# Seven block products instead of eight in other chunks of the feed-forward parts of a two-layer hybrid block

## The chip, the cores and the metric

The kernel runs on one core of one Trainium2 chip. The metric is the device time of one execution in microseconds, as a median of several runs. It has five engines that matter here: TensorE (PE, with its weight loads shown as PEld), VectorE (DVE), ScalarE (ACT), GpSimd (POOL, hardly used) and SyncE (SP), which issues the transfers.

## What is computed

Two layers work on two streams of 256 tokens each (the latent and the context) with a width of 1024. A layer has a feed-forward part, a mixer of three branches and a second feed-forward part. Every part is preceded by a normalization whose shift, scale and gate come from a conditioning vector (`ada_w`). Cut to the parts that the change touches:

```python
def swiglu(h, w1, w3, w2):
    return (jax.nn.silu(h @ w1) * (h @ w3)) @ w2
...
for l in range(DEPTH):
    ml = (sc @ ada_w[l] + ada_b[l]).reshape(B, 1, N_MOD, D_MODEL)
    mc = (scc @ ada_w[l] + ada_b[l]).reshape(N_MOD, D_MODEL)
    xl = xl + 0.5 * ml[:, :, 2] * swiglu(ln_mod(xl, ...), ffn_w1[l, 0], ffn_w3[l, 0], ffn_w2[l, 0])
    xc = xc + 0.5 * mc[2] * swiglu(ln_mod(xc, ...), ffn_w1[l, 0], ffn_w3[l, 0], ffn_w2[l, 0])
    yl, yc = token_mixer(...)
    xl = xl + ml[:, :, 5] * yl
    xl = xl + 0.5 * ml[:, :, 8] * swiglu(ln_mod(xl, ...), ffn_w1[l, 1], ffn_w3[l, 1], ffn_w2[l, 1])
    ...
```

`h @ w1` and `h @ w3` go from 1024 to 2816 columns, `w2` goes back. All arithmetic is in fp32.

## The kernel before

Activations lie transposed: 128 features on the partitions, 512 columns for the tokens of both streams (the first 256 latent, `LAT`, the others context, `CTX`). Every fp32 operand of the large products is split into a high and a low part of the faster type fp32r, and a product takes three matmuls (high by high, high by low, low by high). The splitting of weights is done on the chip: ScalarE casts the high part (line 253 or 662), VectorE subtracts it (line 254 or 663).

A feed-forward part (`ffn`, line 708, named here by layer and part as (0,0), (0,1), (1,0) and (1,1)) goes over the 22 chunks of 128 columns of `w1` and `w3` in three thirds (`THIRDS`, line 25: chunks 0 to 7, 8 to 14, 15 to 21). A chunk ends with silu, product and split into `gh` and `gl`; after each third follow its downs, eight products with `w2` that are added to `x`. The last downs of a part go by stream, so that the next normalization can begin.

A normal chunk loads its weights (`load13`), splits them and multiplies 8 blocks of 128 rows of `w1` and `w3` by all 512 columns: 2 x 8 x 3 = 48 matmuls of 512 columns. The other form (`seven`, line 652) regards `w1`, `w3`, the two halves of the inner dimension and the two streams as 2 by 2 blocks and takes seven block products instead of eight: 7 x 4 x 3 = 84 matmuls of 256 columns. For that VectorE makes block sums of the weights in place (line 674), each of the seven blocks is split anew (lines 662 and 663), and the results are combined on VectorE. The block sums of the moving operand (`seven_sums`, line 634) are made once in a part; the code calls it three chunks (`SUMS`) ahead of the first seven, and the results are given back after the last one. They take 16 of the 27 tiles (`W_FFN`) in which split weights are held; one more holds the junk output of line 394.

`SEVEN` (line 37) says which chunks take that form. Three of the four parts have such chunks.

The modulation of later stages is computed beside the feed-forward parts by VectorE: `ada_steps` (line 377) multiplies tiles of `ada_w`, 512 KB each, by the conditioning vector and sums along the columns (line 394), for each tile once per stream, with two tiles in flight. These steps are handed out by `feed`: in normal chunks that aren't the last of their third, two rates' worth, and in each down of the first two thirds, one rate. The rate divides the number `FEEDS` of a part (42, 40, 40 tiles) by the number of these places (`ups`, line 715, counts the chunks). `lazy` gives the steps a priority 300 places later than their place in the code.

PE's order is that of the code (line 97). On the other engines and on SP a planner orders the instructions at build time by priority and by when it holds their operands to be ready; each engine then works through its list in order.

```python
units = SEVEN.get((l, j), ())
ups = sum(m not in units and m < b - 1 for a, b in THIRDS for m in range(max(a, 3), b))
rate = FEEDS.get((l, j), 0) / (2 * ups + 16)
```

Of the kernel before, what the change touches and what calls it, by code (L numbers as in the profile page):

```python
# [33 lines left out]
FEEDS = {(0, 0): 42, (0, 1): 40, (1, 0): 40}  # L34


SEVEN = {(0, 0): range(8, 16), (0, 1): range(8, 16), (1, 0): range(8, 22)}
SUMS = 3
PREP = 3
LATER = 300  # L40
# [48 lines left out]
def body(ctx, tc, ins, out):  # L89
# [618 lines left out]
    def ffn(l, j, streams, order, after, first, ahead, prep=None):  # L708
# [4 lines left out]
        filled = False  # L713
        units = SEVEN.get((l, j), ())
        ups = sum(m not in units and m < b - 1 for a, b in THIRDS for m in range(max(a, 3), b))
# [1045 lines left out]
```

## Time and profile before

| | us |
|---|---|
| median of 3 runs (2202.43 to 2210.25) | 2202.67 |
| the profiled execution | 2201.5 |
| its span, from the first to the last instruction | 2199.7 |
| PE busy in the span | 2139.0 (97%) |
| DVE busy | 1642.8 (75%) |
| ACT busy | 1121.1 (51%) |
| mean granted clock of TensorE | 0.995 |

A busy time is the union of the durations of an engine's instructions. Matmuls overlap in the records, so the pace of a row of them is read from the length of a stretch and not from the single duration. [...]

### The profile page before, as it was taken

What the parts mean: (1) busy time and instruction counts of PE and PEld (TensorE: products, weight loads), DVE (VectorE), ACT (ScalarE), POOL (GpSimd) and SP (SyncE); (2) the same over time, 40 slices, a digit from 0 to 9 for tenths busy, and PEclk for the clock granted to TensorE, in tenths of its full rate; (3) what the DMA queues carried; (4) which work ended last, traced back from release to release, by engine and by line L of the source; (5) the groups of instructions that cost most, each with busy time, mean ns of one, the idle gap of its engine ahead of it and who ended that gap; (6) DMA issues with size and microseconds to landing.
All of it is one profiled execution on the core that took longest, in us unless ns stands there. A gap on an engine that the chain in (4) does not pass through costs nothing.

```text
span 2199.7 us, 35090 instructions
## 1 busy us (share of the span) xinstructions
PE 2139.0 (97%) x13405; PEld 1877.3 (85%) x13405; DVE 1642.8 (75%) x3455; ACT 1121.1 (51%) x2265; POOL 26.7 (1%) x59
## 2 busy tenths in 40 slices
PE   6999899999999999999989999999999999999999
PEld 5778888977787778998888889899999778999999
DVE  6899994568776644699997359797785987868664
ACT  4425443558676533442344344245454878757553
POOL 0000000000000000000000000000000000000000
PEclk9999999999999999999999999999999999999999
DMA  9563463311122333336535324753242222454652
GB/s 361 189 230 137 163 222 104 111 67 63 68 62 92 103 100 104 117 134 221 174 124 180 126 87 145 252 188 106 96 154 95 66 99 82 149 188 167 234 190 95
DMA packets 73658, 310.44 MB, mean 141 GB/s; under 512 B 6929, under 2 KB 10513, under 8 KB 59025
## 3 DMA queue, kind: packets, MB, share of 16 engines
q1 hardware_dynamic: 73488, 308.19, 40.1%
q8 instruction: 105, 1.72, 0.3%
q14 instruction: 65, 0.52, 0.1%
HBM read 303.97 MB, written 4.19 MB: 140 GB/s over the span
## 4 chain that ended last, share of the span: by engine, by line
PE 82%; DVE 10%; ACT 4%; DMA 2%; issue 1%; POOL 0%; SPq 0%; ACTq 0%; DVEq 0%; POOLq 0%
PE dn L268 6%; PE dn L269 6%; PE dn L270 6%; PE p L268 6%; PE p L269 6%; PE p L270 6%; PE pg L268 3%; PE pg L269 3%; PE pg L270 3%; PE pj L268 2%; PE pj L269 2%; PE pj L270 2%; PE pa L669 2%; DVE wlo L663 2%; PE pa L667 2%; PE pa L668 2%
## 5 line engine op out<-in xcount | busy, mean ns | idle before, releaser
L253 ACT CAST whi<-raw 128x512 fp32r<-128x512 f32 x724 | 431.5, 610 | 551.0 <-PE p L269 160.5
L254 DVE TENSOR_TENSOR wlo<-raw,whi 128x512 fp32r<-128x512 f32 x724 | 480.0, 675 | 259.1 <-ACT whi L253 177.9
L268 PE MATMUL dn<-gh,whi 128*128 128x512 f32 (+1 forms) x809 | 275.6, 341 | 0.0
L269 PE MATMUL dn<-gl,whi 128*128 128x512 f32 (+1 forms) x809 | 275.1, 340 | 0.0
L270 PE MATMUL dn<-gh,wlo 128*128 128x512 f32 (+1 forms) x809 | 275.0, 340 | 0.0
L394 DVE SCALAR_TENSOR_TENSOR junk<-ada,cb 128x1024 bf16<-128x1024 f32 x208 | 253.6, 1219 | 26.6 <-DMA ada<-ada 25.1
L268 PE MATMUL p<-hh,whi 128*128 128x512 f32 (+1 forms) x736 | 256.3, 348 | 0.0
L269 PE MATMUL p<-hl,whi 128*128 128x512 f32 (+1 forms) x736 | 256.1, 348 | 0.1
L270 PE MATMUL p<-hh,wlo 128*128 128x512 f32 (+1 forms) x736 | 255.7, 347 | 0.0
L662 ACT CAST whi<-raw 128x512 fp32r<-128x512 f32 x210 | 129.7, 621 | 149.0 <-DVE raw L674 56.3
L270 PEld LDWEIGHTS dn<-gh,wlo 128*128 128x128 f32 x809 | 152.2, 188 | 18.7
L269 PEld LDWEIGHTS dn<-gl,whi 128*128 128x128 f32 x809 | 152.1, 188 | 18.6
L268 PEld LDWEIGHTS dn<-gh,whi 128*128 128x128 f32 x809 | 152.1, 188 | 18.6
L268 PEld LDWEIGHTS p<-hh,whi 128*128 128x128 f32 x736 | 138.4, 188 | 20.8 <-ACT whi L253 0.8
L268 PE MATMUL pj<-hh,whi 128*128 128x512 f32 (+1 forms) x400 | 154.2, 385 | 1.9 <-DVE li L941 1.9
L270 PEld LDWEIGHTS p<-hh,wlo 128*128 128x128 f32 x736 | 138.4, 188 | 19.4
L269 PEld LDWEIGHTS p<-hl,whi 128*128 128x128 f32 x736 | 138.4, 188 | 19.2 <-DVE hl L495 0.3
L663 DVE TENSOR_TENSOR wlo<-raw,whi 128x512 fp32r<-128x512 f32 x210 | 140.1, 684 | 12.0 <-ACT whi L662 11.8
L269 PE MATMUL pj<-hl,whi 128*128 128x512 f32 (+1 forms) x400 | 144.0, 360 | 0.0
L270 PE MATMUL pj<-hh,wlo 128*128 128x512 f32 (+1 forms) x400 | 143.7, 359 | 0.0
L268 PE MATMUL pg<-hh,whi 128*128 128x512 f32 (+1 forms) x384 | 130.0, 339 | 0.0
L269 PE MATMUL pg<-hl,whi 128*128 128x512 f32 (+1 forms) x384 | 129.7, 338 | 0.0
(341 smaller groups left out, 5006.4 us busy)
## 6 DMA issues: line engine op xcount, KB each, us to landing
raw<-w SPq DMA_DIRECT2D x104, 1024.0 KB, 5.0
ada<-ada SPq DMA_DIRECT2D x124, 512.0 KB, 3.8
raw<-win SPq DMA_DIRECT2D x30, 1024.0 KB, 4.9
raw<-w SPq DMA_DIRECT2D x32, 896.0 KB, 4.6
raw<-wbr SPq DMA_DIRECT2D x24, 1024.0 KB, 4.8
raw<-wbo SPq DMA_DIRECT2D x24, 512.0 KB, 3.6
raw<-wout SPq DMA_DIRECT2D x8, 1024.0 KB, 4.9
raw<-ada SPq DMA_DIRECT2D x6, 1024.0 KB, 7.2
```

The lines of the kernel that those rows point to most:

```text
L253: S.copy(hi[:, :e], r[:, a:a + e])
L254: V.tensor_tensor(lo[:, :e], r[:, a:a + e], hi[:, :e].bitcast(F32), op=ALU.subtract)
L268: PE.matmul(o, hi[:, ws], xh[k][:, cols], start=(k == 0), stop=False)
L269: PE.matmul(o, hi[:, ws], xl[k][:, cols], start=False, stop=False)
L270: PE.matmul(o, lo[:, ws], xh[k][:, cols], start=False, stop=(k == kk - 1))
L394: V.scalar_tensor_tensor(junk[0][:, :D], r, 1.0, cb[0][:, s * D:(s + 1) * D], op0=ALU.mult, op1=ALU.mult, accum_out=am[:, b, s:s + 1])
L662: S.copy(hi[:, :T], src)
L663: V.tensor_tensor(lo[:, :T], src, hi[:, :T].bitcast(F32), op=ALU.subtract)
L667: PE.matmul(o, hi[:, ws], xh[:, cols], start=(first and i == 0), stop=False, skip_group_check=True)
L668: PE.matmul(o, hi[:, ws], xl[:, cols], start=False, stop=False, skip_group_check=True)
L669: PE.matmul(o, lo[:, ws], xh[:, cols], start=False, stop=(i == KD // 2 - 1), skip_group_check=True)
```

## The change

Part (0,0) takes the form with seven products for chunks 15 to 21 (7 chunks) instead of 8 to 15 (8 chunks), part (0,1) for chunks 12 to 21 (10) instead of 8 to 15 (8). Part (1,0) keeps chunks 8 to 21. With that the call of `seven_sums` moves from chunk 5 to chunk 12 in (0,0) and to chunk 9 in (0,1), and the places of `feed` and its rate follow.

```diff
-SEVEN = {(0, 0): range(8, 16), (0, 1): range(8, 16), (1, 0): range(8, 22)}
+SEVEN = {(0, 0): range(15, 22), (0, 1): range(12, 22), (1, 0): range(8, 22)}
```

## Rows read from the trace of the kernel before

**Rows 1.** The page: busy time by engine, and the chain that ended last by engine.

```profile
PE 2139.0 (97%) x13405; PEld 1877.3 (85%) x13405; DVE 1642.8 (75%) x3455; ACT 1121.1 (51%) x2265; POOL 26.7 (1%) x59
...
PE 82%; DVE 10%; ACT 4%; DMA 2%; issue 1%; POOL 0%; SPq 0%; ACTq 0%; DVEq 0%; POOLq 0%
```

**Rows 2.** Stretches: length, busy PE, PEld, DVE, ACT, POOL, clock, DMA share, GB/s.

```profile
127.28:171.90 44.62, 44.62 (x195) 36.15 (x194) 42.57 (x80) 10.34 (x17) 0.00 (x0) 1.00 0.59 210
171.90:256.06 84.16, 74.68 (x590) 71.82 (x589) 82.33 (x153) 43.38 (x89) 0.00 (x0) 0.98 0.40 140
256.06:295.03 38.97, 38.97 (x170) 31.54 (x169) 37.47 (x71) 10.10 (x18) 0.00 (x0) 1.00 0.62 213
295.03:304.96 9.93, 9.93 (x85) 9.92 (x84) 9.68 (x19) 6.83 (x14) 0.00 (x0) 1.00 0.45 161
304.96:371.94 66.98, 66.98 (x290) 54.09 (x289) 37.49 (x63) 23.72 (x42) 0.00 (x0) 1.00 0.46 158
966.03:1021.87 55.84, 55.84 (x243) 45.09 (x242) 52.72 (x95) 18.76 (x32) 0.00 (x0) 1.00 0.54 181
...
1066.43:1156.57 90.14, 78.59 (x590) 75.12 (x588) 84.88 (x157) 43.59 (x89) 0.00 (x0) 0.94 0.39 136
1156.57:1195.51 38.94, 38.94 (x170) 31.53 (x169) 27.94 (x54) 11.89 (x19) 0.00 (x0) 1.00 0.54 189
1195.51:1205.49 9.98, 9.98 (x86) 9.97 (x84) 7.63 (x16) 7.13 (x15) 0.00 (x0) 1.00 0.30 106
1205.49:1272.44 66.95, 66.95 (x291) 54.09 (x289) 27.52 (x43) 23.23 (x42) 0.00 (x0) 1.00 0.34 120
...
1449.60:1520.54 70.94, 70.53 (x590) 69.83 (x588) 67.77 (x126) 42.99 (x89) 0.00 (x0) 1.00 0.35 121
...
1559.57:1629.13 69.56, 69.56 (x589) 69.55 (x588) 64.03 (x118) 45.16 (x94) 0.00 (x0) 1.00 0.29 101
```

**Rows 3.** The same table for a stretch of normal chunks without modulation steps.

```profile
338.50:349.70 11.20, 11.20 (x50) 9.04 (x49) 3.79 (x6) 3.41 (x7) 0.00 (x0) 1.00 0.25 86
```

**Rows 4.** The same table for line 394 alone: DVE's busy time (records) in each stretch.

```profile
171.90:256.06 84.16, 21.65 (x36) 0.98 0.40 140
256.06:295.03 38.97, 20.84 (x34) 1.00 0.62 213
295.03:304.96 9.93, 1.23 (x2) 1.00 0.45 161
304.96:371.94 66.98, 11.04 (x18) 1.00 0.46 158
...
1066.43:1156.57 90.14, 24.50 (x40) 0.94 0.39 136
1156.57:1195.51 38.94, 8.59 (x14) 1.00 0.54 189
...
1449.60:1520.54 70.94, 4.78 (x8) 1.00 0.35 121
...
1559.57:1629.13 69.56, 0.00 (x0) 1.00 0.29 101
```

**Rows 5.** Timeline of DVE in the middle third of (0,0): start, length, instruction.

```profile
208.87 1.22 DVE L394 SCALAR_TENSOR_TENSOR junk<-ada,cb 128x1024 bf16<-128x1024 f32 x1
...
210.02 0.69 DVE L663 TENSOR_TENSOR wlo<-raw,whi 128x512 fp32r<-128x512 f32 x1
```

**Rows 6.** Waits of PE in 1066.43 to 1156.57: total us, times, longest.

```profile
PE pa L667 <- ACT whi L662: 5.6, 6, 1.0
PE pa L669 <- DVE wlo L663: 3.7, 6, 0.7
```

**Rows 7.** The same table for the sums' tiles alone, part (0,1): DVE, ACT busy.

```profile
947.00:976.00 29.00, 16.01 (x32) 4.85 (x8) 1.00 0.29 100
```

**Rows 8.** Timeline of DVE in the last third of (1,0).

```profile
1569.84 0.68 DVE L663 TENSOR_TENSOR wlo<-raw,whi 128x512 fp32r<-128x512 f32 x1
1570.44 0.68 DVE L674 TENSOR_TENSOR raw<-raw 128x512 f32<-128x512 f32 x1
```

## The prediction

> **What bounds the kernel now.** I read the page first, then one table of stretches with the borders of the feed-forward stages, the same table for the modulation steps of line 394 alone, and last the waits and the timeline of one bad stretch. The page says that TensorE is busy for 97% of the span and that the chain which ended last is 82% PE and 10% DVE [rows 1]. So nearly everything lies on TensorE; what is to be won is PE time, and the tenth where PE waits for VectorE.
>
> The table of stretches [rows 2] prices both forms of a chunk. A normal chunk is 66.98 / 6 = 11.16 us on PE in part (0,0) and 55.84 / 5 = 11.17 us in part (0,1). The seven-product form at its best is the last third of part (1,0): 69.56 / 7 = 9.94 us, PE busy throughout. It saves 1.23 us a chunk: 84 matmuls of 256 columns instead of 48 of 512. But the same form in the middle thirds of the first two parts takes 84.16 / 7 = 12.02 us and 90.14 / 7 = 12.88 us, more than the normal form. There the reader should look at the DVE column: 82.33 of 84.16 us busy in the one, 84.88 of 90.14 in the other, while PE is idle for 9.5 and 11.5 us.
>
> Why DVE is full there: a seven-product chunk gives it 64.03 / 7 = 9.15 us of work per 9.94 us [rows 2], a normal chunk only 3.79 us per 11.2 [rows 3]. What else sits in these stretches are the modulation steps of line 394; each shows as two records, the product and the readout of its sum, and a feed makes one tile of two steps, one for each stream. 36 records, 18 steps, 21.65 us lie in the middle third of (0,0), and 20 steps, 24.50 us, in that of (0,1); in (1,0) only 4 are left when its sevens start and none is in its last third [rows 4]. A step is 1.20 us. DVE takes its instructions in order, so in the timeline a split of the weights (line 663) stands behind such a step [rows 5], and the waits of PE in that stretch are for exactly these splits and for the casts that follow DVE's block sums [rows 6]. PE also loses clock: the granted share is 0.94 over the middle third of (0,1) against 1.00 in the last third of (1,0) [rows 2]; after the waits the clock was at the lower of its two levels, which on 90.14 us costs some 5 us.
>
> **The change part by part.** Nothing is computed that was not computed before; the sevens move, and one is added (17 instead of 16 in these two parts). Downs (192 and 168 matmuls, 44.6 and 39.0 us) stay as they are.
>
> (a) Middle third of (0,0), chunks 8 to 14, becomes normal: 84.16 to 7 x 11.17 = 78.2 us, 6.0 less. (b) Last third of (0,0): chunk 15 was a seven already (9.93), 16 to 21 normal (66.98), 76.9 in all [rows 2]; seven sevens without steps take 69.56, 7.3 less. (c) Middle third of (0,1): 8 to 11 normal, 12 to 14 seven: 4 x 11.17 + 3 x 9.94 = 74.5 instead of 90.14, 15.6 less. (d) Last third of (0,1): 9.98 + 66.95 = 76.9 to 69.56, 7.4 less. Together 36.3 us: the ceiling.
>
> What comes off this is where the modulation steps now go. The feeds are written only in normal chunks but the last of a third, and in the downs of the first two thirds. (0,0) has 4 + 6 such chunks instead of 4 + 5, so the rate falls from 42/34 = 1.235 to 42/36 = 1.167; (0,1) has 4 + 4, so it rises from 40/34 = 1.176 to 40/32 = 1.25. All feeds now end with the downs of the second third; before, five chunks of the last third of each part had them. So about the same steps have less room ahead of the last third, and DVE has to fit them in.
>
> The budget of (0,0): after the first third's downs (36 + 34 + 2 + 18) / 2 = 45 of its 84 steps are still to do [rows 4], 45 x 1.20 = 54.0 us. The room is 78.2 + 39.0 = 117.2 us. The rest of DVE's work there is 7 x 3.79 = 26.5 for the chunks, 16.0 for the sums of the moving operand, which move here from the start of the part [rows 7], and 37.47 - 20.84 = 16.6 for the downs [rows 2, 4]: 113.1 us, 96% of the room. DVE is at 95% and 96% in the downs of the first two thirds with PE never idle [rows 2], so this fits, barely; 0 to 6 steps may be left for the first sevens.
>
> The budget of (0,1): (40 + 14) / 2 = 27 steps are still to do after the first downs [rows 4], 32.4 us. Room 74.5 + 38.9 = 113.4; other work 4 x 3.79 + 16.0 of sums + 3 x 9.15 + (27.94 - 8.59) = 78.0 [rows 2 to 4, 7]; sum 110.4, 97%. The sums leave the start of this part too, which frees 16 us ahead, room for 13 steps. The spare of chunks 8 to 11 (44.7 - 15.2 - 16.0) holds ten or so, the downs 15; up to 9 can fall into the sevens 12 to 14.
>
> The price of a step in a seven, from both sides: 4 steps in the middle third of (1,0) cost 70.94 - 69.56 = 1.4 us, 0.35 each; 20 in that of (0,1) cost 20.6, 1.03 each [rows 2, 4]. I take 5 steps at 0.6 in chunks 12 to 14, 3 us (between 0 and 3 x (12.88 - 9.94) = 8.8); 2 us for the last third of (0,0) (0 to 6 steps, 0 to 6 us) and 1 us for that of (0,1) (0 to 3). These lean to the cheap end since few steps meet few sevens, as in (1,0).
>
> The other edits cost nothing while their cover holds. The sums take 16 of the 27 weight slots three chunks ahead of the first seven, so chunks 12 to 14 of (0,0) and 9 to 11 of (0,1), and the downs up to the freeing, run with ten. Chunks 5 to 7 and the first downs do so now, with PE busy for 55.84 of 55.84 and 44.62 of 44.62 us [rows 2]. If that cover fails, chunks 12 to 14 of (0,0) ask DVE for 3 x 3.79 + 16.0 + 2 x 2.33 x 2 x 1.20 = 38.6 us in 33.5, and chunks 9 to 11 of (0,1) for 3 x 3.79 + 16.0 + 3 x 2.5 x 2 x 1.20 = 45.4, unless the steps give way: up to 5 and 12 us. I take 0, since the steps are issued 300 places later in priority and gave way to the sums before: in the chunks that had sums and steps together PE never waited [rows 2]. SP's transfers have room: the busiest of these stretches moves data at a share of 0.62 with PE never idle [rows 2]. The end of the last third is as in (1,0), where its downs follow a seven without a gap.
>
> Sum: 36.3 - 6 = 30.3 us. The profiled execution took 2201.5 us (2199.7 of span and 1.8 around it), 1.2 under the median of 2202.67. 2201.5 - 30.3 + 1.2 = 2172.4; I say 2172.
>
> [...] Two 512-column operations of DVE in a row start 0.60 us apart although each shows 0.68 [rows 8], so a seven needs 9.15 us of DVE and PE stays the bound. [...]
>
> **The rivals.** First, it is slower: the steps fall into the last thirds. The decisive point is how many of a part's 84 and 80 steps are left when its last third begins; at 18 to 20 the sevens run as the middle thirds do now, 84.16 and 90.14 instead of 76.9 and 76.9. That is +7.3 and +13.2; (a) still gives 6.0, (c) with its sevens at 12.88 gives 90.14 - 44.7 - 38.6 = 6.8, net +7.7: 2210. For it speaks that all feeds must now be over two thirds in; against it, that (0,0) had only 10 left at its chunk 15 although five fed chunks with 12 feeds were to come, and that (1,0) ran out of steps by its first seven although the feeds of its second downs are written behind that [rows 4]. 5%.
>
> Second, no change: what PE waits for is DVE's total, and the waits only change place; then only the one seven more counts, 1.2 us: 2200 to 2202. Against it: DVE has idle time in the last thirds now, 37.49 busy of 66.98 and 27.52 of 66.95 [rows 2], which the change fills. 7%.
>
> Third, a half gain: the sums, steps and ten slots together make PE wait in the normal chunks before the sevens, or steps spill into several sevens of the last third. With some 5 and 12 us lost, 2172 + 9 to 2172 + 17: 2181 to 2189. 17%.
>
> Fourth, DVE sets the pace of every seven because its operations don't overlap there: a seven would take 9.15 x 0.68 / 0.60 = 10.4 us [rows 2, 8] against 9.94, 17 x 0.46 = 8 us less gain, 2180. The 9.94 us of (1,0), which hold that overlap, speak against it: 1%. [...]
>
> Forecast, 2165 to 2180, the ceiling included: 70%.
>
> **How the numbers follow.** The predicted time is the forecast's, 2172. The range reaches from the ceiling with some noise (2201.5 - 36.3 + 1.2 = 2166, so 2164) to most of the third rival, 2186; outside lie the first two rivals and the end of the third, about 16%. A measurement of this kernel can tell about 0.5%, 11 us: faster means under 2191.7. The forecast, the third and the fourth are faster, 88%; the second is the same, and a part of the first (under 2213.7), 9%; slower 3%.
>
> **What would show it.** In the profile after: middle third of (0,0) near 78 us with PE never idle; last thirds near 70 each with few or no records of line 394 in them; the sevens 12 to 14 of (0,1) between 30 and 36 us; no wait of PE for wlo beyond a few us; DVE at 95% between the first downs and the last third, and the granted clock 1.00 there. Wrong would be: waits of PE at the normal chunks with sums, or more than ten records of line 394 behind the start of a last third.

## The result and the profile after

The changed kernel takes 2170.2 us (median of 4 runs, 2168.5 to 2172.6) against 2206.5 for the kernel before (4 runs): ratio 0.9837, 95% interval 0.9811 to 0.9863, faster by some 36 us. The four runs of the kernel before reach from 2202.4 to 2210.3 us; in the set of runs in which both kernels were measured once more (below) their medians are 2205.4 and 2172.6, 32.8 apart. The profiled executions, 2201.5 and 2170.2 us, differ by 31.3; the ledger below is made on these.

The table of stretches of the changed kernel, with the borders of the stages answering to those of [rows 2] (length, busy PE, PEld, DVE, ACT, POOL, clock, DMA share, GB/s):

```profile
173.00:251.16 78.16, 78.16 (x338) 63.13 (x337) 76.46 (x141) 24.36 (x41) 0.00 (x0) 1.00 0.52 181
251.16:290.04 38.88, 38.88 (x170) 31.53 (x169) 22.45 (x42) 9.91 (x17) 0.00 (x0) 1.00 0.37 136
290.04:359.52 69.48, 69.48 (x590) 69.48 (x588) 64.06 (x118) 45.20 (x94) 0.00 (x0) 1.00 0.29 101
...
1054.81:1100.66 45.85, 45.08 (x194) 35.92 (x192) 43.66 (x82) 18.10 (x31) 0.00 (x0) 1.00 0.41 138
1100.66:1133.26 32.60, 30.53 (x253) 29.91 (x252) 29.40 (x54) 19.83 (x39) 0.00 (x0) 1.00 0.42 150
...
1172.26:1241.62 69.36, 69.36 (x590) 69.36 (x589) 64.07 (x118) 45.16 (x94) 0.00 (x0) 1.00 0.29 102
```

PE has no idle time in the middle third of (0,0) (78.16 us) and in both last thirds (69.48 and 69.36). DVE is as full as before in the middle third of (0,0), 76.46 of 78.16 us, but beside normal chunks that costs PE nothing. The granted clock, the share of its full speed that TensorE was allowed, is 1.00 where it was 0.98 and 0.94. In the middle third of (0,1) of the kernel before it was 0.50, the lower of the two levels in its records, from 1095.4 to 1097.4 us, behind waits of 1.00 and 0.66 us; matmuls of 256 columns began 0.21 us apart there and 0.12 at 1.00. The same table for line 394 alone:

```profile
67.72:128.46 60.74, 29.48 (x48) 1.00 0.76 275
128.46:173.00 44.54, 23.34 (x38) 1.00 0.60 212
173.00:251.16 78.16, 44.69 (x73) 1.00 0.52 181
251.16:290.04 38.88, 3.17 (x6) 1.00 0.37 136
290.04:359.52 69.48, 0.00 (x0) 1.00 0.29 101
...
1100.66:1133.26 32.60, 3.46 (x6) 1.00 0.42 150
...
1172.26:1241.62 69.36, 0.00 (x0) 1.00 0.29 102
```

No step is left when a last third begins, and three (six records) meet the sevens of the middle third of (0,1), where there were twenty [rows 4]. The ledger:

| stretch | before | forecast | after |
|---|---|---|---|
| (0,0) middle third | 84.16 | 78.2 | 78.16 |
| (0,0) last third | 76.91 | 71.6 | 69.48 |
| (0,1) middle third: chunks 8 to 11 | | 44.7 | 45.85 |
| chunks 12 to 14 | | 32.8 | 32.60 |
| together | 90.14 | 77.5 | 78.45 |
| (0,1) last third | 76.93 | 70.6 | 69.36 |

The four stretches give back 32.7 us; 1.2 of it is lost ahead of them (the first normal chunk begins at 67.7 us instead of 66.5), the rest is level. That start lies between 65.6 and 67.7 us in the profiled runs of this document, with sevens in either place, so the 1.2 us are not shown to come from the change.

### The profile page after: what moved, and what is told of

Same layout as the page of the kernel before. It is cut to its first block, busy times and chain, and to the rows that moved or that the text cites. A ratio compares the mean times of both kernels' runs of the same rounds, so it can differ in the third digit from the quotient of the medians.

```text
span 2168.4 us, 35183 instructions
## 1 busy us (share of the span) xinstructions
PE 2125.3 (98%) x13441; PEld 1871.7 (86%) x13441; DVE 1649.4 (76%) x3466; ACT 1121.3 (52%) x2272; POOL 26.7 (1%) x59
## 4 chain that ended last, share of the span: by engine, by line
PE 80%; DVE 10%; ACT 4%; DMA 3%; issue 2%; POOL 0%; SPq 0%; DVEq 0%; ACTq 0%; POOLq 0%
PE dn L268 6%; PE dn L269 6%; PE dn L270 6%; PE p L268 5%; PE p L269 5%; PE p L270 5%; PE pg L268 3%; PE pg L270 3%; PE pg L269 3%; PE pa L667 2%; PE pa L669 2%; PE pa L668 2%; PE pj L268 2%; PE pj L269 2%; PE pj L270 2%
## 5 line engine op out<-in xcount | busy, mean ns | idle before, releaser
L253 ACT CAST whi<-raw 128x512 fp32r<-128x512 f32 (+1 forms) x720 | 427.8, 610 | 499.6 <-PE dn L269 143.4
L254 DVE TENSOR_TENSOR wlo<-raw,whi 128x512 fp32r<-128x512 f32 (+1 forms) x720 | 476.4, 675 | 218.4 <-ACT whi L253 137.0
L270 PE MATMUL p<-hh,wlo 128*128 128x512 f32 (+1 forms) x720 | 249.5, 347 | 0.8 <-DVE wlo L254 0.8
L268 PE MATMUL p<-hh,whi 128*128 128x512 f32 (+1 forms) x720 | 249.8, 347 | 0.0
L269 PE MATMUL p<-hl,whi 128*128 128x512 f32 (+1 forms) x720 | 249.6, 347 | 0.0
L662 ACT CAST whi<-raw 128x512 fp32r<-128x512 f32 x217 | 134.1, 621 | 112.7 <-PE pa L668 35.2
L663 DVE TENSOR_TENSOR wlo<-raw,whi 128x512 fp32r<-128x512 f32 x217 | 143.9, 685 | 20.7 <-ACT whi L662 20.2
L270 PE MATMUL pg<-hh,wlo 128*128 128x512 f32 (+1 forms) x384 | 129.5, 337 | 0.0
```

The lines of the kernel that those rows point to most:

```text
L253: S.copy(hi[:, :e], r[:, a:a + e])
L254: V.tensor_tensor(lo[:, :e], r[:, a:a + e], hi[:, :e].bitcast(F32), op=ALU.subtract)
L268: PE.matmul(o, hi[:, ws], xh[k][:, cols], start=(k == 0), stop=False)
L269: PE.matmul(o, hi[:, ws], xl[k][:, cols], start=False, stop=False)
L270: PE.matmul(o, lo[:, ws], xh[k][:, cols], start=False, stop=(k == kk - 1))
L662: S.copy(hi[:, :T], src)
```

## The experiments

The theory: a seven leaves VectorE 0.8 us of its 9.9, so where many modulation steps stand beside sevens each delays PE by nearly its own 1.2 us; beside normal chunks it is free. The rivals: only the number of block products counts; or the middle third is a bad place by itself (ten weight slots, the sums, the downs around it).

**One part alone.** In each run one of the two ranges is that of the kernel before.

```diff
-SEVEN = {(0, 0): range(15, 22), (0, 1): range(12, 22), (1, 0): range(8, 22)}
+SEVEN = {(0, 0): range(15, 22), (0, 1): range(8, 16), (1, 0): range(8, 22)}    # e1_only_00
+SEVEN = {(0, 0): range(8, 16), (0, 1): range(12, 22), (1, 0): range(8, 22)}    # e2_only_01
```

> Only part (0,0) is changed (chunks 15 to 21), part (0,1) stays at 8 to 15. Theory (modulation steps on VectorE make the sevens slow): middle third of (0,0) 84.2 to 78.2 us, last third 76.9 to 69.5, together 13.4 us less than before, and the middle third of (0,1) stays near 90. Rival (only the number of block products counts): one seven fewer than before, 1.2 us more.

> Only part (0,1) is changed (chunks 12 to 21), part (0,0) stays at 8 to 15. Theory: middle third of (0,1) 90.1 to 78.5 us, last third 76.9 to 69.4, 19 us less than before, and the middle third of (0,0) stays near 84. If the two parts don't influence each other, this and the run with (0,0) alone add up to the whole 32. Rival (only the number of products counts): two sevens more, 2.5 us less.

The first took 2190.8 us, ratio 0.9932 (0.9911 to 0.9953), the second 2183.7, ratio 0.9902 (0.9887 to 0.9917). Two rows of the first, its middle third of (0,0) and the unchanged one of (0,1), then the unchanged middle third of (0,0) of the second:

```profile
172.80:250.96 78.16, 78.16 (x338) 63.13 (x336) 75.62 (x138) 24.37 (x41) 0.00 (x0) 1.00 0.50 177
...
1052.91:1144.60 91.69, 79.11 (x589) 75.20 (x588) 87.20 (x161) 43.41 (x89) 0.00 (x0) 0.94 0.40 140
```

```profile
171.98:257.62 85.64, 76.16 (x589) 73.28 (x588) 82.35 (x153) 43.38 (x89) 0.00 (x0) 0.96 0.38 135
```

Each part gains in its own stretches, and the middle third of the other stays within 1.6 us of what it was. 1 - 0.9932 and 1 - 0.9902 add up to 1.66%, the whole change has 1.63%. The first run has one seven fewer than the kernel before and is 14 us faster (2190.8 against 2205.0): the number of products doesn't decide.

**The steps made short.** In both kernels each step of line 394 works on 32 of its 1024 columns, so most of the modulation sums is left out; the transfers of the tiles stay.

```diff
-                    V.scalar_tensor_tensor(junk[0][:, :D],
-                                           r, 1.0,
-                                           cb[0][:, s * D:(s + 1) * D],
+                    V.scalar_tensor_tensor(junk[0][:, :32],
+                                           r[:, :32], 1.0,
+                                           cb[0][:, s * D:s * D + 32],
```

> The kernel before with each modulation step of line 394 over 32 of its 1024 columns, so most of the modulation sums is left out; transfers, waits and the place of the steps stay. Theory: the sevens in both middle thirds run as in part (1,0), 69.6 us each instead of 84.2 and 90.1, 35 us less than before, and the granted clock there is 1.00. Rival (the middle third itself is a bad place: ten weight slots, the sums, the downs around it): both stay near 84 and 90, no more than 3 us less.

> The changed kernel with the same short steps of line 394 over 32 of 1024 columns. Theory: it gains only what its three disturbed sevens lost, 1 to 4 us against the changed kernel, and comes out within 2 us of the kernel before with short steps (17 sevens against 16, 1.2 us): without the steps the change is worth next to nothing. Rival (place): it keeps its whole lead of some 30 us over the kernel before with short steps.

The kernel before with short steps took 2175.0 us (2171.1 to 2178.7), ratio 0.9861 (0.9842 to 0.988); the changed one 2166.6 (2165.0 to 2169.6), ratio 0.9824 (0.9808 to 0.9841), both against the kernel before. The rows of the first: middle third of (0,0), first downs of (0,1), middle third of (0,1); and PE's wait in those downs:

```profile
171.97:242.24 70.27, 69.99 (x589) 69.65 (x588) 66.51 (x170) 42.95 (x89) 0.00 (x0) 1.00 0.58 204
1007.86:1056.35 48.49, 46.24 (x194) 37.04 (x192) 26.64 (x98) 10.75 (x18) 0.00 (x0) 0.96 0.76 272
1056.35:1126.07 69.72, 69.72 (x590) 69.65 (x589) 63.22 (x115) 44.61 (x90) 0.00 (x0) 1.00 0.29 101
```

```profile
PE dn L270 <- DVE wlo L254: 2.2, 1, 2.2
```

The table for line 394 in the two middle thirds:

```profile
171.97:242.24 70.27, 5.02 (x52) 1.00 0.58 204
1056.35:1126.07 69.72, 0.00 (x0) 1.00 0.29 101
```

This settles the place: the same sevens in the same middle thirds, with the same sums and ten slots, take 70.3 and 69.7 us instead of 84.2 and 90.1 as soon as the steps are short. In (0,0) more steps than before stand beside the sevens (26 instead of 18), with their transfers, and cost next to nothing: it is their length that counts. In (0,1) the short steps are done before the middle third begins, so that third shows the sevens without any. The two give 34.3 us, as expected; the total fell by 30, since two downs lost 4.9 (48.49 against 44.56, and 45.46 against 44.52 in (1,0)). With the steps short VectorE comes to the head of its queue before their tiles have landed, and a split of weights then waits behind a step that waits for its transfer, here 1.84 us:

```profile
1024.96 0.19 DVE L394 SCALAR_TENSOR_TENSOR junk<-ada,cb 128x32 bf16<-128x32 f32 x1 [1.84 <-DMA ada<-ada]
1025.08 0.08 DVE L394 DVE_READ_ACCUMULATOR junk<-ada,cb 128x1 f32 x1
1025.08 1.66 DVE L559 SCALAR_TENSOR_TENSOR x<-dn,Ga,x 128x256 f32<-128x256 f32 x4
1026.65 1.28 DVE L254 TENSOR_TENSOR wlo<-raw,whi 128x512 fp32r<-128x512 f32 x2
```

The two kernels with short steps should have come out within 2 us and are 8.5 apart in their medians, 5.2 in their profiled executions. There the stages of (0,1) give 3.0 (two sevens more), those of (0,0) take 0.5 back, and such a wait for transfers, about 4 us with the clock it costs (0.96 and 0.97 granted in these stages), sits in (0,1) in the one and in (1,0) in the other. Why the medians lie further apart stays open. Still, of the 33 to 36 us between the kernels 8.5 or fewer are left without the steps.

**Ranges around the chosen ones.** `e5_01_from15` has (0,1) from chunk 15, like (0,0); `e6_00_from12` has (0,0) from chunk 12, like (0,1).

```diff
+SEVEN = {(0, 0): range(15, 22), (0, 1): range(15, 22), (1, 0): range(8, 22)}    # e5_01_from15
+SEVEN = {(0, 0): range(12, 22), (0, 1): range(12, 22), (1, 0): range(8, 22)}    # e6_00_from12
```

> The changed kernel with sevens in part (0,1) only from chunk 15 (7 instead of 10). Theory: chunks 12 to 14 cost 33.5 us instead of 32.6, but the sums move away from chunk 8 and the feeds get room: within 1.5 us of the changed kernel, since three sevens beside a few steps gain 0.9 us instead of 3.7. Rival (only the number of products counts): 3.7 us slower than the changed kernel.

> The changed kernel with sevens in part (0,0) from chunk 12 too (10 instead of 7). Theory: 24 of the 84 steps are still open when chunk 12 begins (18 of them would meet the sevens or the downs), so the three sevens take 33 to 37 us instead of 33.5: 0 to 4 us slower than the changed kernel. Rival (only the number of products counts): 3.7 us faster.

Ratios 0.9855 (0.9841 to 0.987) and 0.9852 (0.9837 to 0.9866), 2171.8 and 2171.6 us, not to be told from the changed kernel. The rows can tell: the middle third of (0,1) of the first, all normal, then chunks 12 to 14 of (0,0) of the second, as sevens, and last its records of line 394 there:

```profile
1055.70:1133.64 77.94, 77.94 (x337) 63.09 (x336) 54.86 (x99) 26.05 (x42) 0.00 (x0) 1.00 0.39 137
```

```profile
217.12:255.81 38.69, 34.45 (x253) 33.22 (x252) 35.86 (x67) 18.64 (x38) 0.00 (x0) 0.91 0.40 140
```

```profile
217.12:255.81 38.69, 11.01 (x18) 0.91 0.40 140
```

With no seven at all this middle third takes 77.94 us, with three 78.45 (76.2 to 81.3 in the profiles of the six other runs with full steps and sevens from chunk 12 in this part): that the three sevens of the change bring anything there is not shown. And three sevens that meet 9 steps take 38.7 us where three normal chunks take 33.5; 38.69 - 29.82 = 8.9 us, 0.99 for each step.

**The feeds handed out late.** The first rival of the prediction, made on purpose, in two versions.

```diff
# e7_late_feeds
+        late = (l, j) == (0, 0)
-        rate = FEEDS.get((l, j), 0) / (2 * ups + 16)
+        rate = 0 if late else FEEDS.get((l, j), 0) / (2 * ups + 16)
...
                     finish(seven(l, j, m, sums), None)
+                    if late:
+                        feed(6)
# e9_forced_late: the same, and
-                if j == 0 or l == 0:
+                if (j == 0 or l == 0) and not late:
...
+            if late and ti == 2:
+                cond_load()
+                filled = True
             while m < b:
```

> The changed kernel, but all 42 feeds of part (0,0) are handed out in the seven sevens of its last third, six in each, none before. This is the first rival of the prediction made on purpose. Theory: the sevens of that third run as the middle thirds before, 12.0 to 12.9 us each with some three steps, 84 to 90 us instead of 69.5; what is left of the steps falls on the downs and the next part; 15 to 40 us slower than the changed kernel, so slower than or equal to the kernel before. Rival (the place decides, not the steps): the last third stays near 70 us.

The first took 2170.0 us, ratio 0.9846 (0.9829 to 0.9863): no change. Line 394 in the same five stretches of (0,0) as above:

```profile
67.60:128.35 60.75, 29.48 (x48) 1.00 0.76 276
128.35:172.89 44.54, 23.34 (x38) 1.00 0.60 213
172.89:251.04 78.15, 42.96 (x70) 1.00 0.50 176
251.04:289.92 38.88, 4.91 (x8) 1.00 0.41 146
289.92:359.40 69.48, 0.00 (x0) 1.00 0.28 101
```

Though all feeds are written in the last third, the steps run where they ran. Neither the rate nor the place of `feed` holds them; that fits a planner which takes a step as soon as it holds the step's tiles to be there and VectorE to be free. So the run tested nothing of the price, but it shows that a budget made from the places of `feed` was no forecast of where steps go. The second version holds them by a dependence.

> The changed kernel, with the 42 feeds of part (0,0) in its seven last sevens and the tile for the junk output of line 394 taken only there, out of the weight slots, so that the steps cannot run before the slot's last reader, a matmul of the downs ahead of these sevens. Handing the feeds out late had left the steps where they were; this holds them back by a dependence. Theory (steps beside sevens cost 0.8 to 1.03 us each): some three steps in each seven, the last third 84 to 90 us instead of 69.5, the rest of the 84 steps in the downs behind it, where some of them delay the norm: 15 to 40 us slower than the changed kernel. Rival (the place in the part decides, not the steps): the last third stays near 70 us.

It took 2248.4 us, ratio 1.0192 (1.0172 to 1.0212): 78 us more than the changed kernel and slower than the one before. Its last third of (0,0), the downs behind it and the next part's first stage, then line 394 in the first of them:

```profile
289.40:400.94 111.54, 87.44 (x590) 83.53 (x589) 104.62 (x190) 44.59 (x92) 0.00 (x0) 0.83 0.41 142
400.94:457.59 56.65, 43.61 (x282) 39.78 (x280) 52.86 (x109) 20.11 (x42) 2.69 (x10) 0.91 0.67 230
457.59:514.30 56.71, 40.51 (x296) 38.32 (x294) 43.73 (x91) 18.62 (x41) 1.66 (x1) 0.82 0.52 178
```

```profile
289.40:400.94 111.54, 46.37 (x75) 0.83 0.41 142
```

The third that ran in 69.5 us takes 111.5 with 38 steps in it, 1.11 us for each; the granted clock falls to 0.83. PE is idle for 24.1 of these 42 us, and its busy time for the same matmuls is 18.0 us longer, so part of this price is the lower clock's. It came out a little above the expected 0.8 to 1.03; the number of steps was well off: I expected three in each seven and there were five, and the rest cost 16.5 us in the downs and 18 in the stage behind.

**The SiLU that runs ahead.** In the changed kernel PE waits once for 1.6 us in chunk 13 of (0,1). The timelines of ScalarE and PE there:

```profile
1116.74 1.91 ACT L369 ACTIVATE cb<-cb 128x2048 f32<-128x2048 f32 x1 [1.63 <-DMA cb<-cB]
1118.56 0.35 ACT L685 COPY c<-pa 128x256 f32<-128x256 f32 x1
```

```profile
1118.97 0.39 PE L667 MATMUL pa<-th,whi 128*128 128x256 f32 x1 [1.61 <-ACT c L685]
```

The steps of (0,1) now end at 1107.6 us, so the conditioning tile is free early, and its load for part (1,0) with the SiLU of line 369 runs ahead into the sevens. An added reader holds it back:

```diff
+            if filled and ti == 2 and l == 0:
+                V.tensor_tensor(cb[0][:, 0:1], cb[0][:, 0:1], gh[-1][:, 0:1].bitcast(F32), op=ALU.add)
```

> The changed kernel with one small VectorE operation behind the third thirds of the first two parts that reads the conditioning tile and the last gh, so that the next load of that tile and its SiLU on ScalarE can't run ahead of the sevens. Theory: the 1.6 us wait of PE in chunk 13 of (0,1), which stands behind that SiLU (1.9 us on ScalarE after 1.6 us of waiting for its transfer), goes, chunks 12 to 14 take 30.5 us instead of 32.6; 1 to 2.5 us faster than the changed kernel if the SiLU finds a free place later, else no change. Rival (the wait is from steps on VectorE): chunks 12 to 14 stay at 32.6.

2169.6 us, ratio 0.9847 (0.9831 to 0.9863): no difference. Chunks 12 to 14, then the middle third of (1,0):

```profile
1097.19:1128.74 31.55, 30.59 (x253) 29.97 (x252) 29.77 (x55) 18.15 (x38) 0.00 (x0) 1.00 0.36 122
1413.97:1488.64 74.67, 71.91 (x589) 71.29 (x588) 70.47 (x130) 43.22 (x90) 0.00 (x0) 0.98 0.34 116
```

The SiLU now runs at 1250 us and that wait is gone, but only 1.1 us of it shows, as 0.7 is waited for another copy of ScalarE instead, and the middle third of (1,0), which had 70.5 us, takes 74.7. Whether the later load did that is open, since the changed kernel itself, profiled once more below, had 73.6 there.

**Steps moved to an earlier part.** (0,1) without sevens in its middle third has room for more steps, and the sevens of (1,0) would be free of them.

```diff
-FEEDS = {(0, 0): 42, (0, 1): 40, (1, 0): 40}
+FEEDS = {(0, 0): 42, (0, 1): 62, (1, 0): 16}
-SEVEN = {(0, 0): range(15, 22), (0, 1): range(12, 22), (1, 0): range(8, 22)}
+SEVEN = {(0, 0): range(15, 22), (0, 1): range(15, 22), (1, 0): range(8, 22)}    # e10_feeds_01
+SEVEN = {(0, 0): range(15, 22), (0, 1): range(15, 22), (1, 0): range(6, 22)}    # e11_feeds_01_10from6
```

> The changed kernel with part (0,1) taking sevens only from chunk 15, like (0,0), and 62 of the tiles instead of 40, so that (1,0) has 16 instead of 38 left. Theory: (0,1) has room for these 28 more steps in its normal chunks 8 to 14 (VectorE busy for 54.9 of 78.0 us in the run with sevens from 15) and in its second downs (19.7 of 38.9), and the sevens of (1,0) meet no step: its middle third 69.6 us instead of 70.5 to 72.4. 1 to 2 us faster than the changed kernel. Rival (steps are free anyway by then): no change in that third.

> As the run before, and part (1,0) takes sevens from chunk 6 instead of 8, since its first third has few steps left. Theory: two more undisturbed sevens, 2 x 1.23 = 2.5 us, so 3 to 5 us faster than the changed kernel, if the sums of the moving operand, now three chunks ahead of chunk 6, find room on VectorE. Rival (VectorE is full in that third): the two sevens take 12 us or more each, no gain.

> The changed kernel once more, to compare the two versions with moved feeds on the same chip: about 2170 us, 0.984 of the kernel before.

Beside each other they took 2168.6 us (ratio 0.9835, 0.9818 to 0.9851), 2168.7 (0.9832, 0.9815 to 0.9848) and 2172.6 for the changed kernel (0.9847, 0.983 to 0.9864). The two lie 0.1% lower, within the intervals; that they beat the change is not shown. Their stages did what was expected in part. The first one's middle thirds of (0,1) and (1,0), then the second one's chunks 3 to 5 and 6 to 7 of (1,0), then the changed kernel's chunks 8 to 11 of (0,1) and middle third of (1,0) in this execution:

```profile
1052.64:1130.58 77.94, 77.94 (x337) 63.10 (x336) 74.36 (x134) 24.36 (x41) 0.00 (x0) 1.00 0.54 188
1417.40:1486.98 69.58, 69.58 (x589) 69.58 (x588) 63.20 (x115) 43.38 (x89) 0.00 (x0) 1.00 0.29 101
```

```profile
1315.13:1350.70 35.57, 33.93 (x146) 26.89 (x145) 29.29 (x52) 12.71 (x22) 0.00 (x0) 1.00 0.61 209
1350.70:1371.57 20.87, 20.10 (x170) 19.89 (x168) 19.46 (x38) 12.34 (x25) 0.00 (x0) 1.00 0.33 124
```

```profile
1054.48:1103.70 49.22, 46.36 (x193) 37.13 (x192) 46.49 (x87) 18.05 (x31) 0.00 (x0) 0.97 0.42 139
1420.97:1494.57 73.60, 71.68 (x589) 71.27 (x588) 70.00 (x130) 43.33 (x90) 0.00 (x0) 0.98 0.34 117
```

35 steps (69 records of line 394) beside normal chunks cost PE nothing (77.94 of 77.94 busy, DVE 74.36), and the sevens of (1,0) without steps take 69.58. The two extra sevens of the second gain nothing: 35.57 + 20.87 = 56.4 us for chunks 3 to 7, where the first needs 55.7.

## Why the prediction was right, and where it was not

The time, 2172 against 2170.2, and its sign follow from the step on which most of it rests: that the sevens of the two middle thirds are slow because modulation steps share VectorE with them. The short steps show it, and the forced late feeds show it from the other side. The fourth rival, that VectorE's operations don't overlap and a seven takes 10.4 us, is excluded: both last thirds of sevens shown above take 69.4 and 69.5 us, 9.9 a chunk.

That the total came so close is in part luck. The gains of (b) and (d) were forecast 3.3 us too low; 0.9 too much in (c) and 1.2 us lost at the start, for which the sum has no term, took most of that back.

(a) was right: 6.0 us. (b) and (d) were too low by 2.1 and 1.2 us, the allowances for steps left over: none was. The budget of (0,0) put DVE at 96% up to the last third, with 0 to 6 steps left, while 82 of the 84 were done by 251 us and the second downs had two-fifths of their time free (22.45 of 38.88). What failed is the count of what was already done: the sums had left the start of the part, and I did not let the freed time there take steps. It did: 45 steps were done by 173 us, 43 of them in the two stretches shown, where the prediction had counted 39 (84 less the 45 still to do [rows 4]). Over the middle third and its downs together, for which the budget said 96%, DVE was busy for 98.9 of 117.0 us, 85%: 98% of the first and 58% of the second. The sign named for it (95% up to the last third) did not come.

(c) came out at 11.7 us, forecast 12.6. Chunks 12 to 14 lost 2.8 us, forecast 3, but by another cause: three steps, not five, and 1.6 us of it behind the SiLU of line 369, of which the prediction says nothing. Chunks 8 to 11 lost 1.2 us that were taken at nothing (the cover of ten slots and sums): 0.8 are waits of PE for splits of weights. This is a wait at normal chunks with sums, which the prediction named as a sign of being wrong; it is the mechanism of the third rival, only small. The prediction's reason was that steps gave way to the sums. No step stands among them here either, but the sums themselves stand on VectorE in front of the splits (the last section shows it in the execution where it cost most). The rows of part (0,1) from which the cover was read held less than half of the sums, 6.6 of 16 us; the rest lay in the stage ahead of them. In the changed kernel 10.5 us fall into the first 11.2 us of chunk 8. The table for the sums' tiles (DVE, ACT), before and after:

```profile
966.03:1021.87 55.84, 6.63 (x15) 2.83 (x5) 1.00 0.54 181
```

```profile
1054.81:1066.00 11.19, 10.48 (x24) 3.67 (x6) 1.00 0.01 1
```

The price of a step beside sevens was taken at 0.6 us, between 0.35 and 1.03. Where many meet, it is the upper end or above: 0.99 and 1.11 in the two runs that crowd them. The mechanism by which the first rival would come, feeds written late, moves nothing by itself, so its 5% were too many for this kernel; its price was far too low: held by force, in one part alone, it made the kernel 43 us slower than before (1.0192), where the prediction had a net 8 for both parts, since 38 steps met the sevens and not 18 to 20, and because those left over were to cost nothing in the downs and the norm behind.

The second rival (waits only change place) fell: PE's idle time in these four stretches went from 21.0 to 2.8 us. The third has the shape of what was seen in (0,1), at 1.2 us and not 9 to 17.

## What to carry to other kernels

A form that saves the bound engine work and gives the next engine more of it is best placed where that next engine has no other work; here the same seven products took 9.9 us, or 12 to 16 where modulation steps of full length stood among them in VectorE's queue. Read the price of such a form from a stretch where it runs alone, and the price of company from one where it doesn't, before counting operations. Where a planner orders the queues, the place of background work in the code is not where it runs: look at its records in the trace, and hold it by a dependence if it has to stay.

## What the runs showed that was not expected

A wait of 2.86 us had a price by the clock as well. The changed kernel profiled a second time has one wait of PE in chunks 8 to 11 of (0,1), and that stretch lasts 49.22 us instead of 45.85. Two lines of VectorE in front of it, the wait, and the row of the time in which the granted clock was low:

```profile
1068.03 0.42 DVE L642 SCALAR_TENSOR_TENSOR ts<-ts,ts 128x256 f32<-128x256 f32 x1
1068.36 0.69 DVE L254 TENSOR_TENSOR wlo<-raw,whi 128x512 fp32r<-128x512 f32 x1
```

```profile
1069.11 0.50 PE L270 MATMUL p<-hh,wlo 128*128 128x512 f32 x1 [2.86 <-DVE wlo L254]
```

```profile
1069.99:1073.40 3.41, 3.41 (x10) 2.64 (x9) 3.41 (x6) 1.46 (x3) 0.00 (x0) 0.50 0.00 0
```

VectorE was never idle from the start of the stretch to this split and worked on the sums for 13.2 of these 13.9 us. Behind the wait the granted clock was 0.50 for 3.4 us. PE's busy time for the same matmuls rises from 45.08 to 46.36, 1.3 us, on top of 2.1 us more of waiting. Not every wait of PE cost clock: the one of 1.61 us in chunk 13, shown above, left it at 1.00.

The two executions of the same code differ by 5.5 us of span (2168.4 and 2173.9); this stretch and the middle third of (1,0), 73.60 against 70.49 with one wait of 1.9 us, account for 6.5 of it, the rest goes the other way. Differences of that size between two variants are so not to be read from one execution.
